# Cross-covariance attention: seventeen of the last eighteen stores issued from GpSimd's queue instead of SyncE's

## The chip, the cores and the metric

The kernel runs on one core of a Trainium2 chip. The metric is the device time of one execution in microseconds; the kernel before takes 128.43 us, the median of three runs. Engines are named as the profile names them: PE is TensorE, PEld its weight loads, DVE VectorE, ACT ScalarE, POOL GpSimd and SP SyncE. Sixteen DMA engines move data between HBM and the on-chip memory SBUF; any of several engines' queues can issue a transfer to them.

## The reference

Q, K and V have the shape (8, 12, 512, 64) in float32: 96 heads of 512 tokens by 64 features. Attention is between features, not tokens, so each head's attention matrix is 64x64.

```python
Q_norm = Q / (np.linalg.norm(Q, axis=-2, keepdims=True) + 1e-10)
K_norm = K / (np.linalg.norm(K, axis=-2, keepdims=True) + 1e-10)
attn = np.einsum('bhnd,bhne->bhde', Q_norm, K_norm)
attn = np.exp(attn - np.max(attn, axis=-1, keepdims=True))
attn = attn / (np.sum(attn, axis=-1, keepdims=True) + 1e-10)
return np.einsum('bhnd,bhde->bhne', V, attn).astype(np.float32)
```

Each of the three inputs and the output is 12.58 MB, so 50.3 MB cross between HBM and SBUF.

## The kernel before

The 96 heads are worked through in 24 units `u` of four heads, 12 pairs of units `s`, and 6 groups `w` of two pairs. For each pair, q and k are loaded in float32, cast to bfloat16 side by side (`cast_qk`, L213, DVE), and multiplied with themselves on PE (`grams`, L233), which gives the product of q and k together with their squared norms. From that come the norms (`squares`, `sums`, `powers`), the k side scaled by its norm (`scale_k`, L263, key `sc`, on POOL or DVE), a transposition (`logits`), the exponentials with the q side's norm as scale (`exps`, ACT) and the normalised attention in bfloat16 (`normalise`, L291).

V goes its own way: for each group it is loaded (`load_v`, key `lv`, L194 for a whole MB and L196 for the last one, which comes in two halves), cast to bfloat16 (`cast_v`, key `cv`, L170 on POOL and L168 on DVE), transposed on PE (`vtrans`, key `vt`, L302) and copied out of PSUM (`vcopy`, key `vc`). With both at hand, PE makes the output (`outs`, key `ou`, L319), four parts `x` for each pair; each part is copied to SBUF (`ocopy`, key `oc`, L166 on ACT, L168 on DVE) into the tile `so[s, i]`, of which a pair has two. There are 13 buffers for `so`. Each of the 24 tiles is 512 KB and is written to HBM by `store`, key `st`. I number the stores 2s + i, from 0 to 23. A store's rows in HBM are runs of 2 KB, two for each of 128 partitions.

Two stores have a form of their own. Number 19, (s, i) = (S - 3, 1), called `FEW`, is cut into four transfers (L204, L205) by partitions. Number 23, the last, is written in two halves with the keys `sh` and `st` (L457, L458), the first as soon as its first part is copied; its rows are then runs of 1 KB.

The order of all this isn't left to a scheduler: the class `Order` holds every piece of work with the engines it may run on, a planned cost, the pieces that it must come after (their ends) and behind (their beginnings), and a rank. `run` steps through a planned time, takes the piece that can begin first, or among those within 0.05 us the one of lowest rank, and gives each engine its program in that order. On the chip each engine then works in order, waiting at each instruction for what it needs. Transfers are pieces of the planned engine `DMA`, which means SP's queue: loads and stores stand there in one order, with up to 8 in flight (`QUEUE`). A store's rank is its place in the output plus `ST_LAG` (1.51), above the ranks of the loads, so that loads go first when both can.

The lines in question, L453 to L460: the stores, each behind the one before it. `S` is 12 and `W` 6; `BOTH` is 4, the pair from which DVE may help with the output copies.

Of the kernel before, what the change touches and what calls it, by code (L numbers as in the profile page):

```python
# [13 lines left out]
D = 64  # L14
# [88 lines left out]
def kernel(  # L103
# [7 lines left out]
    nc = tc.nc  # L111
# [3 lines left out]
    S = U // 2  # L115
    W = S // 2
# [3 lines left out]
    HELD, UNTIL = ("lk", 1, 1), ("cq", 0, 1)  # L120
    BOTH = S - 8
    FEW = (S - 3, 1)

# [9 lines left out]
    Of = out.rearrange("b h n d -> (b h n d)").rearrange(  # L135
        "(w r e i p x) -> w e i p r x", r=2, e=2, i=2, p=128, x=J * D)
# [25 lines left out]
    qk32, v32, vb, qkb, gram, scr, kq, n2, r8, kqs, rq, lg, ex, ab, vps, vt, po, so = ({} for _ in range(18))  # L162
# [26 lines left out]
    def load_v(w, r, c):  # L189
        if (w, r) not in v32:  # L190
            v32[w, r] = vp.tile([128, 2, T * D], F32, name="v32")
        o, i = v32[w, r], Vu[w, r].rearrange("p (c x) -> p c x", c=2)
        if c is None:
            nc.sync.dma_start(out=o.rearrange("p c x -> p (c x)"), in_=Vu[w, r])  # L194
        else:
            nc.sync.dma_start(out=o[:, c], in_=i[:, c])  # L196

    def store(s, i, k=None):
        rows = slice(None) if k is None else slice(k * (J // 2), (k + 1) * (J // 2))
        o = Of[s // 2, s % 2, i].rearrange("p r (j d) -> p r j d", d=D)  # L200
        if (s, i) == FEW:

            for a, b in ((0, 76), (76, 80), (80, 128)):
                nc.sync.dma_start(out=o[a:b, 0], in_=so[s, i][a:b, 0])  # L204
            nc.sync.dma_start(out=o[:, 1], in_=so[s, i][:, 1])  # L205
            return
        nc.sync.dma_start(out=o[:, :, rows], in_=so[s, i][:, :, rows])
# [151 lines left out]
    X = 1.29  # L359
    R = dict(cq=2.5, gr=2.471, sq=0.756, kq=1, rd=3.457, pw=3.5, sc=1, rq=1.9, lg=5, ex=1.1, nm=2.545, cv=1.165, vt=0.9, vc=1.1, ou=2, oc=0.9)  # L360
    BIAS = dict(sc=-0.6, kq=5, cv=1, vc=-0.3, oc=0.6)
    QK_PACE, V_FROM, V_PACE, ST_LAG = 0.631, 0.0377, 0.7486, 1.5133

    def v_at(v):
        return V_FROM + V_PACE * v / U

    def piece(key, engines, after, behind, rank, fn, *args):
        if key[0] in ("cv", "vc", "oc", "kq", "sc"):
            plan.add(key, engines, after, behind, rank, lambda eng: fn(eng, *args))
        else:  # L370
            plan.add(key, engines, after, behind, rank, lambda eng: fn(*args))

    def back(kind, i, n, *rest):
        return (kind, i - n, *rest) if i - n >= 0 else None
# [9 lines left out]
    for s in range(S):  # L384
        free = [back("cq", 2 * s + r, 2 * NB["qk"], x) for r in range(2) for x in range(2)]
        for r in parts(s):
            at = QK_PACE * (2 * s + (r or 0)) / U
# [4 lines left out]
    for u in range(U):  # L392
        s, r = divmod(u, 2)
# [17 lines left out]
    def turns(w):  # L411
        return [(q, f) for q in range(4) for f in ((0, 1) if w == W - 1 and q >= TAIL else (None,))]

    last, turned = None, None
    for w in range(W):
        both = 2 * w >= BOTH
        for r in range(2):
            halves = (0, 1) if (w, r) == (W - 1, 1) else (None,)
            n = 2 * w + r - NB["v"]
            for c in halves:  # L420
                free = [("cv", n // 2, n % 2, h) for h in range(2)] if n >= 0 else []
                piece(("lv", w, r, c), {"DMA": X if c is not None else 2 * X}, free, [last], v_at(4 * w + 2 * r + (c or 0)), load_v, w, r, c)
                last = ("lv", w, r, c)
            for c in range(2):
                free = [("vt", w - NB["vb"], *t) for t in turns(w - NB["vb"])] if w >= NB["vb"] else []
                piece(("cv", w, r, c), {"POOL": 1.15, "DVE": (0.72, BIAS["cv"])} if both else {"POOL": 1.15},
                      [("lv", w, r, c if len(halves) == 2 else None)] + free, [("cv", w, r, 0)] if c else [], R["cv"] + 0.01 * (4 * w + 2 * r + c), cast_v, w, r, c)
        for n, (q, f) in enumerate(turns(w)):
            if f is None:
                before = turns(w)[n - 1] if n else turns(w - 1)[-1] if w else None  # L430
                wait = [("vc", w if n else w - 1, *before)] if before else []
            else:
                wait = [("kq", S - 1)] + ([("vc", w, *turns(w)[n - 4])] if n >= 4 and turns(w)[n - 4][1] is not None else [])
            piece(("vt", w, q, f), {"PE": 0.6 if f is not None else 0.8}, [("cv", w, r, c) for r in range(2) for c in range(2)] + wait, [turned],
                  R["vt"] + 0.02 * w, vtrans, w, q, f)
            turned = ("vt", w, q, f)
            copies = {"ACT": 0.74 if f is not None else 1.31}
            if both:
                copies["DVE"] = (0.74 if f is not None else 1.42, BIAS["vc"])
            free = [("ou", 2 * (w - NB["vt"]) + e, x) for e in range(2) for x in range(4)] if w >= NB["vt"] else []  # L440
            piece(("vc", w, q, f), copies, [("vt", w, q, f)] + free, [("vc", w, *turns(w)[n - 1])] if n else [], R["vc"] + 0.02 * w, vcopy, w, q, f)
    for s in range(S):
        for x in range(4):
            i, k = divmod(x, 2)
            n = 4 * s + x - 2
            wait = [("oc", n // 4, n % 4)] if n >= 0 else []
            order = [("ou", s, x - 1) if x else back("ou", s, 1, 3)]
            piece(("ou", s, x), {"PE": 0.5}, [("vc", s // 2, *t) for t in turns(s // 2) if t[0] // 2 == k] + [("nm", s)] + wait, order, R["ou"] + 0.01 * s, outs, s, x)
            n = 2 * s + i - NB["so"]
            free = [("st", n // 2, n % 2)] if k == 0 and n >= 0 else []  # L450
            order = [("oc", s, x - 1) if x else back("oc", s, 1, 3)]
            piece(("oc", s, x), {"ACT": 0.6, "DVE": (0.68, BIAS["oc"])} if s >= BOTH else {"ACT": 0.6}, [("ou", s, x)] + free, order, R["oc"] + 0.01 * s, ocopy, s, x)
        for i in range(2):  # L453
            order = [("st", s, 0) if i else back("st", s, 1, 1)]
            if (s, i) == (S - 1, 1):

                piece(("sh", s, i), {"DMA": 0.67}, [("oc", s, 2)], order, v_at(2 * s + i) + ST_LAG, store, s, i, 0)  # L457
                piece(("st", s, i), {"DMA": 0.67}, [("oc", s, 3)], [("sh", s, i)], v_at(2 * s + i) + ST_LAG, store, s, i, 1)  # L458
            else:
                piece(("st", s, i), {"DMA": X}, [("oc", s, 2 * i), ("oc", s, 2 * i + 1)], order, v_at(2 * s + i) + ST_LAG, store, s, i)  # L460

    ahead = [loaded(x, 0, r) for r in range(2) for x in range(2)]
    held, passed = [], False
# [40 lines left out]
```

## Time and profile before

| | us |
|---|---|
| median of 3 runs (128.43, 128.66, 128.43) | 128.43 |
| the profiled execution | 128.57 |
| its span, first to last instruction | 126.8 |
| PE busy in the span | 79.6 (63%) |
| DVE busy | 91.5 (72%) |
| ACT busy | 72.6 (57%) |
| POOL busy | 36.3 (29%), 40 instructions |
| mean granted TensorE clock | 0.77 of full speed |
| moved by DMA over the span | 50.64 MB, mean 399 GB/s |

A busy share is an average over the whole span; no compute engine is above three quarters. The mean DMA rate has to be held against the rate in the middle of the span, where nothing starts or ends. Issuing a transfer isn't counted as busy time of the engine whose queue issues it, so SP has no busy time and POOL's 36.3 us are its casts and scalings. POOL issues no transfer in this kernel: SP issues all but two, which ACT issues at the start.

In views of single instructions, times are microseconds from the start of the span, and the name of an engine with a q behind it (SPq) is its queue: instructions that issue transfers, wait or synchronise. The views "DMA issues" give the time from the beginning of an issue to the last byte's receipt.

### The profile page before, as it was taken

What the parts mean: (1) busy time and instruction counts of PE and PEld (TensorE: products, weight loads), DVE (VectorE), ACT (ScalarE), POOL (GpSimd) and SP (SyncE); (2) the same over time, 40 slices, a digit from 0 to 9 for tenths busy, and PEclk for the clock granted to TensorE, in tenths of its full rate; (3) what the DMA queues carried; (4) which work ended last, traced back from release to release, by engine and by line L of the source; (5) the groups of instructions that cost most, each with busy time, mean ns of one, the idle gap of its engine ahead of it and who ended that gap; (6) DMA issues with size and microseconds to landing.
All of it is one profiled execution on the core that took longest, in us unless ns stands there. A gap on an engine that the chain in (4) does not pass through costs nothing.

```text
span 126.8 us, 4887 instructions
## 1 busy us (share of the span) xinstructions
PE 79.6 (63%) x2128; PEld 65.1 (51%) x2128; DVE 91.5 (72%) x141; ACT 72.6 (57%) x220; POOL 36.3 (29%) x40
## 2 busy tenths in 40 slices
PE   0064394895964779868574998696575898472000
PEld 0054372774843658656462886485464786361000
DVE  3254749939899399899896898999999799740000
ACT  4000441549688077786792788694748979974000
POOL 4005307300735903033065203223363270300000
PEclk9999655568599555899997569959999689755555
DMA  3999999999999999999999999999999999999993
GB/s 102 399 439 406 432 410 420 416 424 416 423 425 414 417 417 421 408 412 428 426 412 413 416 418 424 414 428 423 399 416 408 406 400 406 401 408 405 408 377 139
DMA packets 15629, 50.64 MB, mean 399 GB/s; under 512 B 1144, under 2 KB 1656, under 8 KB 14200
## 3 DMA queue, kind: packets, MB, share of 16 engines
q1 hardware_dynamic: 15320, 49.29, 96.5%
q10 hardware_dynamic: 288, 1.05, 2.1%
q8 instruction: 16, 0.26, 0.7%
q14 instruction: 5, 0.04, 0.1%
HBM read 37.75 MB, written 12.58 MB: 397 GB/s over the span
## 4 chain that ended last, share of the span: by engine, by line
DMA 36%; DVE 31%; PE 14%; ACT 5%; issue 4%; SPq 1%; DVEq 0%; ACTq 0%
DMA qk<-in_Q_dram 21%; DMA qk<-in_K_dram 15%; DVE qkb L213 11%; PE gram L233 8%; DVE scr L240 6%; DVE ab L291 4%; DVE vb L168 3%; PE po L319 3%; DVE vt L168 2%; DVE n L252 2%; PE vps L302 2%; ACT so L166 2%; ACT ex L282 1%; DVE so L168 1%; ACT kq L166 1%
## 5 line engine op out<-in xcount | busy, mean ns | idle before, releaser
L233 PE MATMUL gram<-qkb 32*128 32x128 bf16 (+1 forms) x1504 | 37.4, 263 | 19.7 <-DVE qkb L213 7.5
L233 PEld LDWEIGHTS <-qkb 32*128 32x128 bf16 (+1 forms) x1504 | 31.6, 118 | 24.2 <-DVE qkb L213 8.8
L213 DVE CAST qkb<-qk 128x1024 bf16<-128x1024 f32 x48 | 35.7, 766 | 8.8 <-DMA qk<-in_Q_dram 6.8
L170 POOL TENSOR_SCALAR vb<-v 128x1024 bf16<-128x1024 f32 x19 | 21.2, 1128 | 44.9 <-DMA v<-in_V_dram 35.0
L166 ACT COPY so<-po 128x512 f32<-128x512 f32 x45 | 24.8, 593 | 6.4 <-PE po L319 6.3
L166 ACT COPY vt<-vps 128x1024 bf16<-128x1024 bf16 (+1 forms) x18 | 17.8, 987 | 16.2 <-PE vps L302 16.2
L319 PE MATMUL po<-ab,vt 128*64 128x128 bf16 x384 | 21.2, 256 | 5.2 <-DVE ab L291 1.5
L302 PE MATMUL vps<-identb,vb 128*128 128x128 bf16 x192 | 18.0, 246 | 6.3 <-POOL vb L170 2.9
L263 POOL TENSOR_TENSOR kqs<-kq,r 64x512 f32<-64x512 f32 x12 | 13.8, 1147 | 26.9 <-ACT r L259 13.8
L240 DVE SCALAR_TENSOR_TENSOR scr<-gram,eye 64x512 f32<-64x512 f32 x24 | 16.5, 688 | 5.5 <-PE gram L233 5.2
L319 PEld LDWEIGHTS <-vt 128*64 128x64 bf16 x384 | 15.5, 130 | 9.6 <-issue 5.1
L302 PEld LDWEIGHTS <-vb 128*128 128x128 bf16 x192 | 13.4, 109 | 9.8 <-POOL vb L170 3.8
L282 ACT ACTIVATE ex<-lg,rq 128x64 f32<-128x64 f32 x48 | 14.5, 322 | 2.6 <-PE lg L276 2.3
L166 ACT COPY kq<-gram 64x512 f32<-64x512 f32 x12 | 7.0, 582 | 13.5 <-DVE scr L240 13.2
L291 DVE TENSOR_TENSOR ab<-ex,rinv 64x256 bf16<-64x256 f32 x24 | 13.8, 573 | 0.6
L282 ACT ACTIVATION_READ_ACCUMULATOR ex<-lg,rq 128x1 f32 x48 | 10.2, 213 | 0.0
L276 PE MATMUL lg<-eye,kqs 64*128 64x64 f32 x48 | 6.4, 259 | 4.2 <-POOL kqs L263 2.8
L252 DVE TENSOR_REDUCE n<-scr 128x8 f32<-128x512 f32 x12 | 8.1, 678 | 0.1
L168 DVE CAST vb<-v 128x1024 bf16<-128x1024 f32 x5 | 7.0, 1403 | 1.4 <-DMA v<-in_V_dram 1.3
L168 DVE COPY vt<-vps 128x1024 bf16<-128x1024 bf16 (+1 forms) x8 | 7.9, 1020 | 0.1
L276 PEld LDWEIGHTS lg<-eye,kqs 64*128 64x128 f32 x48 | 4.5, 156 | 6.0 <-POOL kqs L263 3.5
L288 DVE RECIPROCAL rinv<-esum 128x4 f32<-128x4 f32 x12 | 2.1, 172 | 2.7 <-ACT ex L282 2.5
(17 smaller groups left out, 15.9 us busy)
## 6 DMA issues: line engine op xcount, KB each, us to landing
v<-in_V_dram SPq DMA_DIRECT2D x11, 1024.0 KB, 17.0
out_dram<-so SPq DMA_DIRECT2D x22, 512.0 KB, 10.2
qk<-in_Q_dram SPq DMA_DIRECT2D x8, 1024.0 KB, 17.4
qk<-in_K_dram SPq DMA_DIRECT2D x8, 1024.0 KB, 17.4
qk<-in_Q_dram SPq DMA_DIRECT2D x8, 512.0 KB, 11.9
qk<-in_K_dram SPq DMA_DIRECT2D x6, 512.0 KB, 12.5
qk<-in_K_dram ACTq DMA_DIRECT2D x2, 512.0 KB, 7.4
v<-in_V_dram SPq DMA_DIRECT2D x2, 512.0 KB
```

What stands on the lines that cost most here:

```text
L166: nc.scalar.copy(o, i)
L168: nc.vector.tensor_copy(o, i)
L170: nc.gpsimd.tensor_scalar(out=o, in0=i, scalar1=1.0, scalar2=0.0, op0=ALU.mult, op1=ALU.add)
L213: nc.vector.tensor_copy(qkb[u][:, :, x * D:(x + 1) * D], qk32[s][:, x, r])
L233: nc.tensor.matmul(gram[s][:, h, r, 0], x, x, start=(t == 0), stop=(t == (T if u < WIDE else J) - 1))
L240: nc.vector.scalar_tensor_tensor(out=scr[s][half], in0=gram[s][half, :, :, 0, half].rearrange("p h r d -> p (h r) d"), scalar=1e-20, in1=e ...
L263: (nc.vector if eng == "DVE" else nc.gpsimd).tensor_tensor(out=kqs[s][HI], in0=kq[s][HI], in1=r8[s][HI, :, None].to_broadcast([D, 2 * HU, ...
L276: nc.tensor.transpose(l[:, h, :], kqs[s][HI, 2 * h:2 * h + 2].rearrange("p r d -> p (r d)"), eye2[HI])
L282: nc.scalar.activation(e[:, h, :], lg[s][:, h, :], AF.Exp, scale=rq[s][:, h:h + 1], accum_out=z[:, h:h + 1])
L291: nc.vector.tensor_tensor(out=a[half, :, half], in0=e[half], in1=ri[half, :, None].to_broadcast([D, HU, D]), op=ALU.mult,)
L302: nc.tensor.transpose(ps[:, c, n, :], vb[w][:, J * c + j].rearrange("p r d -> p (r d)"), identb)
L319: nc.tensor.matmul(po[s, x][e * D:(e + 1) * D, j].rearrange("p r d -> p (r d)"), v, ab[s][:, h, :])
```

## The change

The stores numbered 6 to 23, except 19, are issued from POOL's queue by a new function `soft`, whole, 23 included. Stores 0 to 5 and 19 stay on SP's queue with `store`. Each store is behind the one before it on the same queue. The first on POOL's queue, number 6, is behind the scaling of K of pair S - 3 = 9, and number 9 is also behind the last piece of the last cast of V, so that 6, 7 and 8 may stand ahead of that cast and the others may not. In the plan a store on POOL costs 0.75 us of POOL's time, with no flight time and no bound on how many are in flight. Everything else is as it was.

```diff
     FEW = (S - 3, 1)
+    SOFT = 6
...
+    def soft(s, i):
+
+        nc.gpsimd.dma_start(out=Of[s // 2, s % 2, i].rearrange("p r (j d) -> p r j d", d=D), in_=so[s, i])
...
+    stored = {"DMA": None, "POOL": ("sc", S - 3)}
     for s in range(S):
...
         for i in range(2):
-            order = [("st", s, 0) if i else back("st", s, 1, 1)]
-            if (s, i) == (S - 1, 1):
-
-                piece(("sh", s, i), {"DMA": 0.67}, [("oc", s, 2)], order, v_at(2 * s + i) + ST_LAG, store, s, i, 0)
-                piece(("st", s, i), {"DMA": 0.67}, [("oc", s, 3)], [("sh", s, i)], v_at(2 * s + i) + ST_LAG, store, s, i, 1)
+            done, eng = [("oc", s, 2 * i), ("oc", s, 2 * i + 1)], "POOL" if 2 * s + i >= SOFT and (s, i) != FEW else "DMA"
+            order, at = [stored[eng]], v_at(2 * s + i) + ST_LAG
+            if eng == "POOL":
+                if 2 * s + i == SOFT + 3:
+                    order.append(("cv", W - 1, 1, 1))
+                piece(("st", s, i), {"POOL": 0.75}, done, order, at, soft, s, i)
             else:
-                piece(("st", s, i), {"DMA": X}, [("oc", s, 2 * i), ("oc", s, 2 * i + 1)], order, v_at(2 * s + i) + ST_LAG, store, s, i)
+                piece(("st", s, i), {"DMA": X}, done, order, at, store, s, i)
+            stored[eng] = ("st", s, i)
```

## The prediction

> **What bounds the kernel now.** I read the DMA queues first.
>
> ```profile
> q1 hardware_dynamic: 15320, 49.29, 96.5%
> q8 instruction: 16, 0.26, 0.7%
> ```
>
> Each row is packets, MB and packet time as a share of 16 DMA engines over the 126.8 us span. One queue, SyncE's (SP's), fills the engines almost throughout. Then the rate by stretch (last columns: granted TensorE clock, DMA share, GB/s):
>
> ```profile
> 60.00:90.00 30.00, 22.60 (x602) 18.09 (x600) 26.99 (x40) 21.23 (x61) 8.81 (x8) 0.83 1.02 419
> ...
> 112.00:116.00 4.00, 2.57 (x38) 1.95 (x34) 0.30 (x1) 3.15 (x6) 0.00 (x0) 0.50 1.05 405
> 116.00:120.00 4.00, 0.00 (x0) 0.00 (x0) 0.00 (x0) 0.00 (x0) 0.00 (x0) 0.50 1.05 407
> ...
> 122.00:124.00 2.00, 0.00 (x0) 0.00 (x0) 0.00 (x0) 0.00 (x0) 0.00 (x0) 0.50 0.90 341
> 124.00:125.00 1.00, 0.00 (x0) 0.00 (x0) 0.00 (x0) 0.00 (x0) 0.00 (x0) 0.50 0.74 262
> 125.00:126.00 1.00, 0.00 (x0) 0.00 (x0) 0.00 (x0) 0.00 (x0) 0.00 (x0) 0.50 0.18 60
> ```
>
> 419 GB/s where loads dominate, 405 to 407 where only stores run, no computing after 116, and from 122 on the 16 engines run dry one after another: the first is done some 3 us before the last, at about 125.5. So the DMA engines that end last set the end, and computing has slack. Third, who issues what, near the change:
>
> ```profile
> 86.62 1.85 SPq L183 DMA_DIRECT2D qk<-in_K_dram  x1
> 89.11 3.12 SPq L196 DMA_DIRECT2D v<-in_V_dram  x2
> 92.99 17.06 SPq L207 DMA_DIRECT2D out_dram<-so  x14
> 110.83 2.75 SPq L204 DMA_DIRECT2D out_dram<-so  x3
> 114.53 0.37 SPq L205 DMA_DIRECT2D out_dram<-so  x1
> 115.86 4.78 SPq L207 DMA_DIRECT2D out_dram<-so  x5
> ```
>
> The columns are start, duration, line, operation, count. All loads are issued by 92.3; behind them stand 19 stores, numbers 5 to 23 (19 is the one in four pieces, 23 the one in halves). Last, GpSimd (POOL) and the last copies to `so`:
>
> ```profile
> 96.13 1.04 POOL L263 TENSOR_TENSOR kqs<-kq,r 64x512 f32<-64x512 f32 x1 [2.04 <-issue]
> 100.52 2.23 POOL L170 TENSOR_SCALAR vb<-v 128x1024 bf16<-128x1024 f32 x2 [3.35 <-DMA v<-in_V_dram]
> 102.83 1.09 POOL L263 TENSOR_TENSOR kqs<-kq,r 64x512 f32<-64x512 f32 x1
> 107.70 1.04 POOL L263 TENSOR_TENSOR kqs<-kq,r 64x512 f32<-64x512 f32 x1 [3.78 <-ACT r L259]
> ...
> 114.56 1.07 ACT L166 COPY so<-po 128x512 f32<-128x512 f32 x2 [0.24 <-PE po L319]
> ```
>
> POOL has one scaling of K at 96.13, the two last casts of V at 100.52, two more scalings, and is otherwise idle. The last output tile is complete at 115.63, 10 us before the data ends: that is the cover under everything below.
>
> **What the change removes.** SP loses 17 whole stores' issues, 5 and 19 staying (17 whole L207 issues, less store 5, is 16 removed, and the pair of halves of 23 as the 17th). SP's time costs nothing: it waits on its own queue, 10.2 us in all, for earlier stores to land. Stores 0 to 5 and all loads keep their order, and no moved store may begin ahead of the scaling at 96.13, so up to 96 us I expect no difference. Store 23 becomes one transfer. By the issue rows, a store issued at 118.43 landed 6.0 us later (124.4), the first half of 23, issued at 119.71, 5.4 us later (125.1): 0.7 us for a half against 1.3 for a whole, so 2 x 0.7 - 1.3 = -0.1 us. Bounds 0 and -0.1.
>
> **The transfer itself.** 524,288 B at 405 GB/s is 1.295 us a store, 17 make 22.0 us. No row shows a data transfer from POOL's queue. Bounds: at the rate of the stretch with loads (419) each is 0.043 us shorter, 17 x 0.043 = -0.7 us; at the poorest row of another queue, q8's (0.26 MB in 0.7% of 16 x 126.8 = 14.2 us of engine time, 18.5 GB/s each, 295 for sixteen), 8.91 MB take 30.2 us, +8.2. The nearest row is the same stores over SP's queue, so I take 0.
>
> **POOL's issue.** Call it e a store. SP's unblocked issue takes 0.37; its longest, with the queue full, 3.50. Nearest by engine is one pass of POOL over a tile, 1.04 to 1.13, and I take 1.05. Three issues from 97.2 (end of the scaling) end at 100.3, just ahead of the casts' 100.52: cost 0. At 0.37 also 0; at 3.50 they end at 107.7, and all of POOL moves by 7.2.
>
> During these issues VectorE is 2.71 us busy of the 3.30 between 97.20 and 100.50, 1.97 of it in the three casts of q and k. Here a rule speaks against the change: the Trainium skill, "SBUF — State Buffer", section "SBUF: two separate sides", says that a DMA issued from GpSimd has its descriptors written by GpSimd's cores, which VectorE's fp32 copies inside SBUF lock out of a shared port; it gives about 3.1 us for such a DMA beside one and 0.62 alone. If all three early stores met that, they would end at 97.2 + 9.3 = 106.5 by the page. No row here shows a software-issued DMA beside a cast; after 99.94 VectorE has no such cast left.
>
> **The casts of V.** The K load of 86.62 landed 12.5 us after its issue, at 99.1, and store 5, issued at 92.99, 9.9 after, at 102.9; so the second V half, ahead of that store, is in at about 101.6. The early stores now share the engines with it from about 98.2. If the queues take turns packet by packet, 4 KB of V against 2 KB of store, the 3.4 us left of V become up to 1.5 times that: +1.7, V at 103.3, the casts done at 103.3 + 1.1 = 104.4 instead of 102.75. TensorE's transposes of these V, the copies, the output matmuls and the last copy follow, 115.63 + 1.65 = 117.3. Behind the casts POOL's next scaling slips too, and a store ahead of the last scaling can add one e: 118.3. A last store issued then starts by 119.4 and takes 1.3; the engines hold work until 122 to 125.5. So 0, while the tail slips by less than about 4 us; beyond that each us is a us.
>
> **The gap.** While POOL casts, nobody issues stores. The engines that end last have in hand store 5 (102.9) and three early ones: 102.9 + 3 x 1.295 = 106.8, less some 0.3 for the receipt, 106.5. POOL: casts to 104.4, the scaling that already waits (1.09) to 105.5, store 9's issue to 106.55, first bytes perhaps 0.9 later (SP's first issue ended near 1.1 and the engines moved 12 GB/s between 1 and 2 us, 250 between 2 and 3): 107.45. Gap: about 0.9 us at worst order, 0 if the store goes ahead of the scaling or V is delayed less. The engines that end early have 3 us of slack for it. I take +0.5. From there POOL issues 14 stores and one scaling: 105.5 + 14 x 1.05 + 1.04 = 121.2, plus 0.9 and 1.3 is 123.4, inside the 125.5; one store per 1.05 us outruns 1.295.
>
> **The end.** From the last data (125.5) to the span's end stand 1.3 us of waits and clearing. POOL now has its own queue to close: 0 to +0.5 us (its longest drain here, 1.14, bounds it above); I take +0.1.
>
> **Sum.** -0.1 + 0 + 0 + 0.5 + 0.1 = +0.5 us on the profiled execution's own 128.57 (span 126.8 plus 1.8 around it): 129.07. The runs' median, 128.43, lies 0.14 below, so the forecast is **129.0**, range of its own 128.7 to 129.9.
>
> **Rivals.** *Faster (0.32):* packets from the new queue go at 419 GB/s, beside or without loads. For it: the engines sustain that with larger packets, and the new queue has its own descriptors; against: same engines, same 2 KB rows. It gives -0.7 - 0.1 with no gap on the slowest engines: 127.6. It decides from a store time of about 1.26 us on.
> The Trainium skill, "DMA: Bandwidth & Descriptors", section "Issuing engines are not separate DMA queues", denies it: all issuers share the same 16 engines and only issue time is saved; by that the term is 0.
>
> *POOL becomes the bound (0.13):* with e over 1.2 the last store starts too late: 105.5 + 14e + 1.04 + 0.9 + 1.3 passes 125.5 at e = 1.2. At 1.35 that is 14 x 0.15 = +2.1 on top of the 0.5: 131.0. For it: e is unseen, and POOL is in order, so a store that waits for its tile holds back a scaling. Against: POOL is idle 71% of the span and its plain passes take 1.05.
>
> *No difference (0.13):* no gap, the end as before: -0.1 + 0.1, 128.4. For it: bytes and engines are the same, and the bound is DMA.
>
> *Forecast (0.42).* So slower by over 0.2% has 0.42 + 0.13 = 0.55, faster 0.32, within 0.2% (0.26 us, about what a measurement of this kernel can tell from no change) 0.13. The range takes the faster case and POOL's up to e = 1.35: 127.5 to 131.0.
>
> **What would show it.** SP: no store between store 5 and store 19. The V halves landing after 101.6 and the casts after 100.52 show the sharing; the time between early landings of POOL's stores, 1.295 or not, decides the rate; the DMA share near 105 to 108 below 1.0 shows the gap; stretches with only stores should keep 405. I am wrong if stores run at 419 or clearly under 405, if e exceeds 1.2, or if the DMA share never dips and the end moves all the same.

## The result

The changed kernel takes 130.44 us (130.24 to 130.60, four runs), the kernel before in the same runs 128.55: a ratio of 1.0149, 95% interval 1.0136 to 1.0161, or 1.9 us slower. The forecast was 129.0, range 127.5 to 131.0: the direction is right and the range holds the time, but the +0.5 us should have been +1.9. The forecast's own range, 128.7 to 129.9, does not hold it.

First the DMA queues of the kernel after (packets, MB, share of 16 engines over its span of 128.8 us):

```profile
q1 hardware_dynamic: 10424, 40.37, 77.1%
q0 software_dynamic: 2448, 8.91, 17.5%
```

POOL's queue is the new row q0. Its 17 stores made 2,448 packets, 144 each, of which 16 are completions: so 128 packets of 4 KB for 512 KB, where SP's queue makes 256 of 2 KB. Unlike SP's, POOL's issues are counted as busy time: its page shows 57 instructions and 50.0 us, against 40 and 36.3 before. Then POOL's instructions (start, duration, line, operation, count):

```profile
95.93 1.04 POOL L268 TENSOR_TENSOR kqs<-kq,r 64x512 f32<-64x512 f32 x1 [2.12 <-issue]
96.92 2.35 POOL L201 DMA_DIRECT2D out_dram<-so  x3
100.43 1.03 POOL L171 TENSOR_SCALAR vb<-v 128x1024 bf16<-128x1024 f32 x1 [1.16 <-DMA v<-in_V_dram]
101.78 1.30 POOL L171 TENSOR_SCALAR vb<-v 128x1024 bf16<-128x1024 f32 x1 [0.32 <-ACT so L167]
103.02 0.77 POOL L201 DMA_DIRECT2D out_dram<-so  x1
103.86 1.03 POOL L268 TENSOR_TENSOR kqs<-kq,r 64x512 f32<-64x512 f32 x1
104.85 5.08 POOL L201 DMA_DIRECT2D out_dram<-so  x7
...
117.82 0.72 POOL L201 DMA_DIRECT2D out_dram<-so  x1 [0.59 <-ACT so L167]
```

An issue takes 0.72 us (the first 0.90), the three early ones end at 99.3, the last at 118.5; between 99.3 and 104.85 only one store is issued. The rate by stretch, the kernel after (last columns: granted clock, DMA share, GB/s):

```profile
100.00:102.00 2.00, 2.00 (x68) 1.58 (x55) 1.58 (x4) 1.90 (x8) 1.26 (x2) 1.00 1.02 408
102.00:104.00 2.00, 0.93 (x24) 0.77 (x22) 1.55 (x3) 0.78 (x4) 1.93 (x3) 1.00 0.93 373
104.00:106.00 2.00, 1.25 (x20) 0.91 (x14) 1.38 (x2) 1.11 (x2) 2.00 (x3) 0.91 0.86 345
106.00:108.00 2.00, 1.94 (x22) 1.74 (x21) 1.72 (x2) 1.95 (x11) 2.00 (x4) 0.50 0.95 377
116.00:118.00 2.00, 0.86 (x13) 0.43 (x8) 0.00 (x0) 1.38 (x3) 0.90 (x2) 0.50 1.01 342
122.00:124.00 2.00, 0.00 (x0) 0.00 (x0) 0.00 (x0) 0.00 (x0) 0.00 (x0) 0.50 1.03 419
124.00:125.00 1.00, 0.00 (x0) 0.00 (x0) 0.00 (x0) 0.00 (x0) 0.00 (x0) 0.50 0.78 320
125.00:126.00 1.00, 0.00 (x0) 0.00 (x0) 0.00 (x0) 0.00 (x0) 0.00 (x0) 0.50 0.38 156
126.00:127.00 1.00, 0.00 (x0) 0.00 (x0) 0.00 (x0) 0.00 (x0) 0.00 (x0) 0.50 0.15 61
```

Four things are to be seen against the kernel before, which ran at 396 to 409 GB/s from 100 to 122: a gap from 102 to 108; a dip at 116 to 118 with the engines busy all the same (share 1.01); 419 GB/s at 122 to 124, where all but 13 packets are those of POOL's stores; and a tail past 126 in which few engines still work. Last, the drains of SP's and POOL's queues at the end (count, shortest/median/longest ns, first and last start), the kernel before and then after:

```profile
L499 POOLq DRAIN  x3: 39/78/1144, 107.7 to 126.5; - x3
L499 SPq DRAIN  x3: 7/7/7, 126.0 to 126.3; - x3
```

```profile
L507 SPq DRAIN  x3: 7/7/7, 127.5 to 128.3; - x3
L507 POOLq DRAIN  x3: 40/102/10254, 117.8 to 128.6; - x3
```

After, POOL's first drain starts at 117.8 and takes 10.25 us, to 128.05, 0.55 after SP is ready. From the last completion record of a transfer to the span's end it is 126.78 - 125.83 = 0.95 us before and 128.83 - 127.30 = 1.53 after. So of 2.05 us of span, 1.47 lie before the last landing and 0.58 behind it.

### The profile page after: what moved, and what is told of

It reads as the page before. It is cut to its first block, busy times and chain, and to the rows that moved or that the text cites. A ratio compares the mean times of both kernels' runs of the same rounds, so it can differ in the third digit from the quotient of the medians.

```text
span 128.8 us, 4877 instructions
## 1 busy us (share of the span) xinstructions
PE 77.1 (60%) x2128; PEld 62.5 (48%) x2128; DVE 93.4 (72%) x141; ACT 72.8 (57%) x220; POOL 50.0 (39%) x57
## 3 DMA queue, kind: packets, MB, share of 16 engines
q0 software_dynamic: 2448, 8.91, 17.5%
q10 hardware_dynamic: 288, 1.05, 2.1%
## 4 chain that ended last, share of the span: by engine, by line
DVE 29%; DMA 20%; PE 15%; POOL 9%; issue 9%; ACT 8%; POOLq 1%; SPq 0%; DVEq 0%; ACTq 0%
DMA qk<-in_Q_dram 20%; DVE qkb L218 14%; PE gram L238 10%; POOL out_dram L201 6%; DVE scr L245 6%; DVE ab L296 5%; ACT vt L167 3%; PE vps L307 2%; ACT ex L287 2%; POOL kqs L268 2%; PE po L324 2%; DVE n L257 1%; PE lg L281 1%; ACT so L167 1%; DVE vb L169 1%
## 5 line engine op out<-in xcount | busy, mean ns | idle before, releaser
L238 PE MATMUL gram<-qkb 32*128 32x128 bf16 (+1 forms) x1504 | 35.4, 255 | 25.7 <-DVE qkb L218 9.4
L238 PEld LDWEIGHTS <-qkb 32*128 32x128 bf16 (+1 forms) x1504 | 29.8, 114 | 30.3 <-DVE qkb L218 12.5
L218 DVE CAST qkb<-qk 128x1024 bf16<-128x1024 f32 x48 | 37.5, 807 | 7.4 <-DMA qk<-in_Q_dram 5.9
L171 POOL TENSOR_SCALAR vb<-v 128x1024 bf16<-128x1024 f32 x19 | 22.4, 1187 | 37.1 <-DMA v<-in_V_dram 36.7
L324 PE MATMUL po<-ab,vt 128*64 128x128 bf16 x384 | 20.7, 247 | 5.3 <-issue 2.4
L324 PEld LDWEIGHTS <-vt 128*64 128x64 bf16 x384 | 14.6, 124 | 10.0 <-issue 5.8
L296 DVE TENSOR_TENSOR ab<-ex,rinv 64x256 bf16<-64x256 f32 x24 | 15.5, 645 | 0.6
L201 POOL DMA_DIRECT2D out_dram<-so x17 | 12.6, 741 | 3.0 <-ACT so L167 3.0
L169 DVE CAST vb<-v 128x1024 bf16<-128x1024 f32 x5 | 5.1, 1023 | 0.1
```

The lines of the kernel that those rows point to most:

```text
L169: nc.vector.tensor_copy(o, i)
L171: nc.gpsimd.tensor_scalar(out=o, in0=i, scalar1=1.0, scalar2=0.0, op0=ALU.mult, op1=ALU.add)
L201: nc.gpsimd.dma_start(out=Of[s // 2, s % 2, i].rearrange("p r (j d) -> p r j d", d=D), in_=so[s, i])
L218: nc.vector.tensor_copy(qkb[u][:, :, x * D:(x + 1) * D], qk32[s][:, x, r])
L238: nc.tensor.matmul(gram[s][:, h, r, 0], x, x, start=(t == 0), stop=(t == (T if u < WIDE else J) - 1))
L296: nc.vector.tensor_tensor(out=a[half, :, half], in0=e[half], in1=ri[half, :, None].to_broadcast([D, HU, D]), op=ALU.mult,)
```

## Experiments

The orders of PE, DVE and ACT are the same in all of these kernels and in both of the case; only POOL's and SP's queues differ. The ratio is to the kernel before in the same runs.

**Store 19 whole, on POOL's queue.**

```diff
-            done, eng = [("oc", s, 2 * i), ("oc", s, 2 * i + 1)], "POOL" if 2 * s + i >= SOFT and (s, i) != FEW else "DMA"
+            done, eng = [("oc", s, 2 * i), ("oc", s, 2 * i + 1)], "POOL" if 2 * s + i >= SOFT else "DMA"
```

> The kernel after, with store 19 whole and on POOL's queue like the others (18 of the last 18). Theory A (the gap at 103 to 106 us takes from the engines their different leads, and then store 19's four pieces put some 1.6 us of extra rows on four engines that no longer lead, which therefore end last): the four engines lose that, the others gain 0.4, the last landing moves from 127.3 to about 126.5, time 129.6 against the 130.44 of the kernel after. Rival B (the uneven store does nothing; what is lost is lost by slower packets while POOL makes descriptors): 130.4 within 0.15.

129.58 us, ratio 1.0087 (1.0074 to 1.0100): 0.86 us less than after, as theory A had it. The four pieces are the first rows of 76, 4 and 48 partitions and then the second rows of all 128. The trace has a completion record from each of the 16 DMA engines for a whole store, but for the pieces of 76 and of 4 partitions only four late ones each. If each piece is split evenly over its engines, four engines carry 19 + 1 + 3 + 8 = 31 rows and the others 11, where a whole store gives each 16; at 84 ns a row that is an estimated 1.3 us more for the four and 0.4 us less for the others. The records, sorted, in us:

```
store 18 (before):       116.55 116.65 116.94 117.09 117.30 117.74 118.13 118.26 119.26 119.34 119.50 119.53 119.55 119.57 119.64 119.65
last store (before):     122.66 122.78 123.21 124.27 124.66 125.01 125.36 125.44 125.46 125.59 125.63 125.66 125.67 125.74 125.75 125.83
store 16 (after):        115.61 115.67 116.19 116.28 116.53 116.55 116.56 116.58 116.60 116.61 116.64 116.68 116.76 116.81 117.22 117.31
last store (after):      124.56 124.94 124.95 125.00 125.00 125.02 125.04 125.61 125.84 125.96 126.04 126.08 126.75 126.82 127.21 127.30
last store (few_whole):  124.56 124.63 125.37 125.45 125.51 125.53 125.54 125.55 125.73 125.77 125.85 125.91 125.92 126.09 126.12 126.20
```

Store 18 is the last ahead of the pieces in the kernel before, store 16 in the kernel after. Before, the engines are 3.1 us apart there; after, only 1.7, and behind the pieces four stand apart at the end, 0.7 to 1.2 us behind the twelfth. With the store whole they don't.

**More or fewer stores ahead of the casts.** For six, stores 9 to 11 are put in front of the first of the two casts in the finished order:

```diff
-    for (emit, eng), (_, _, key, _) in zip(plan.run(), plan.order):
+    steps = list(zip(plan.run(), plan.order))
+    early = [t for t in steps if t[1][2] in [("st", n // 2, n % 2) for n in range(SOFT + 3, SOFT + 6)]]
+    steps = [t for t in steps if t not in early]
+    at = [t[1][2] for t in steps].index(("cv", W - 1, 1, 0))
+    steps[at:at] = early
+    for (emit, eng), (_, _, key, _) in steps:
```

For none:

```diff
-                if 2 * s + i == SOFT + 3:
+                if 2 * s + i == SOFT:
```

> The kernel after, with six of POOL's stores ahead of the last casts of V instead of three; all other engines' orders are as in the kernel after. Theory A: the gap in the DMA share at 103 to 106 us closes, the engines keep their leads, store 19's uneven pieces fill them again: about 129.7 although the casts begin 0.9 us later. Rival B (the gap falls only on engines that have slack): 130.4 within 0.15. Rival C (the later casts push the last tiles out): above 130.6.

> The kernel after, with none of POOL's stores ahead of the last casts of V (store 6 comes after them). Theory A: the gap grows by what three stores bridged, DMA stands still on nearly all engines from about 102.6 to 104, and the end moves by 1 to 2 us: 131.4 to 132.4. Rival B (gaps fall on slack): 130.4 within 0.3.

Six ahead: 129.19 us, ratio 1.0050 (1.0028 to 1.0072). None ahead: 134.22, ratio 1.0460 (1.0436 to 1.0484), twice what theory A allowed. With none ahead, DMA nearly stops:

```profile
100.00:102.00 2.00, 2.00 (x85) 1.74 (x73) 1.04 (x3) 1.95 (x9) 1.25 (x2) 1.00 0.49 189
102.00:104.00 2.00, 1.40 (x28) 0.93 (x24) 1.95 (x3) 1.27 (x6) 1.93 (x3) 1.00 0.09 36
```

The fewer stores ahead, the later the end; that the gap would fall on slack is refuted. But the twelve runs with six ahead spread from 128.39 to 130.09, those of no other kernel over more than 1.02 us; in its profiled run POOL's first store was issued at 98.01, not 96.92, and the share was still 0.99 to 1.00 at 104 to 108, so the gap was not quite closed there. Nor were the leads quite kept: at store 16 the engines were 2.0 us apart, against 3.1 where store 19 is whole as well.

**Both edits, and store 19 whole on SP's queue.** To six ahead, the edit of the first experiment; or this, so that 19 stays on SP's queue in one piece:

```diff
-        if (s, i) == FEW:
+        if FEW is None:
```

> Six of POOL's stores ahead of the last casts of V and store 19 whole on POOL's queue: both edits of the two kernels before in one. Theory A (store 19's four pieces harm only where the gap has taken the leads of the four engines): with the leads kept, the pieces help, so leaving them out costs, and this is 0.3 us or more slower than the 129.19 with six ahead alone: 129.5 to 130. Rival B (the pieces harm beside POOL's queue whatever the leads): the two gains of 0.9 and 1.25 us add up, about 128.4.

> Six of POOL's stores ahead of the casts, and store 19 whole on SP's queue (with six ahead alone it stands there in four pieces). If the dip at 116 to 118 us and its cost come from the uneven pieces beside POOL's queue, the dip goes and the time is that of store 19 whole on POOL's queue, 128.9 to 129.0. If two queues at work together are the cause, the dip stays and the time is that of six ahead, 129.2 or more.

128.94 us (1.0031, 1.0019 to 1.0043) and 128.89 (1.0029, 1.0017 to 1.0040). Neither theory of the first had it: the pieces neither help nor cost a full 0.9 here; leaving them out gains 0.25, within the spread of six ahead. The second settles the dip: with store 19 whole there is none, on either queue. The same three stretches, 102 to 108, 108 to 114 and 114 to 119, first for the kernel before:

```profile
102.00:108.00 6.00, 5.12 (x93) 4.12 (x88) 5.89 (x8) 5.04 (x19) 2.14 (x3) 0.95 1.05 403
108.00:114.00 6.00, 3.83 (x56) 3.21 (x58) 3.44 (x9) 5.07 (x18) 0.74 (x1) 0.62 1.05 404
114.00:119.00 5.00, 1.01 (x16) 0.73 (x15) 0.00 (x0) 1.39 (x3) 0.00 (x0) 0.50 1.05 407
```

then for store 19 whole but the gap open:

```profile
102.00:108.00 6.00, 3.98 (x50) 3.24 (x51) 4.27 (x7) 3.61 (x13) 5.93 (x8) 0.73 0.90 357
108.00:114.00 6.00, 4.39 (x57) 3.57 (x55) 4.72 (x10) 4.61 (x19) 5.46 (x7) 0.50 1.02 404
114.00:119.00 5.00, 3.04 (x42) 2.25 (x39) 0.55 (x2) 3.46 (x6) 2.91 (x4) 0.50 1.02 395
```

then six ahead, with the pieces:

```profile
102.00:108.00 6.00, 5.09 (x92) 4.09 (x93) 3.87 (x7) 3.85 (x9) 5.83 (x8) 0.86 1.01 404
108.00:114.00 6.00, 3.56 (x68) 2.79 (x67) 5.33 (x11) 5.91 (x27) 4.51 (x6) 0.99 1.02 401
114.00:119.00 5.00, 2.77 (x39) 1.86 (x34) 0.33 (x1) 3.23 (x6) 2.91 (x4) 0.50 1.02 380
```

and six ahead with store 19 whole on SP's queue:

```profile
102.00:108.00 6.00, 4.67 (x49) 3.65 (x50) 3.37 (x5) 3.58 (x13) 5.92 (x8) 0.58 1.03 414
108.00:114.00 6.00, 4.58 (x77) 3.57 (x76) 4.76 (x11) 5.74 (x22) 3.47 (x5) 0.85 1.03 414
114.00:119.00 5.00, 1.18 (x24) 0.73 (x23) 0.00 (x0) 2.06 (x4) 2.18 (x3) 0.77 1.03 415
```

The gap takes the first stretch, the pieces beside POOL's queue the last, and where neither is, the stores run at 414 GB/s, above the 403 to 407 of the kernel before. The kernel after has 365, 400 and 365 in them.

**The pieces in the kernel before.** Store 19 is whole on SP's queue:

```diff
-    FEW = (S - 3, 1)
+    FEW = None
```

> The kernel before with store 19 whole on SP's queue. If the four pieces serve to fill four engines that lead by 1.2 us and more by then, leaving them out costs: the last engines get 0.4 us more, 128.9 against 128.46. If they serve nothing: 128.4.

128.87 us, ratio 1.0028 (1.0018 to 1.0039): as expected, the pieces are worth 0.36 us there. So the right base for the queue change alone is 128.87, and six ahead with store 19 whole, 128.94, is the same kernel but for POOL's queue and the whole last store.

**The pieces elsewhere.** To six ahead: store 5, the last on SP's queue ahead of POOL's, is cut up, and 19 is whole on POOL's.

```diff
-    FEW = (S - 3, 1)
+    FEW = (2, 1)
```

> Six of POOL's stores ahead of the casts; the store in four pieces is number 5, the last on SP's queue, instead of 19, which is whole on POOL's. With the pieces out of the time in which POOL's queue works, the dip to 343 GB/s at 116 to 118 us should go. If the dip costs time, 128.7 or less; if it falls on engines with slack, 129.2 as with six ahead.

128.59 us, ratio 1.0008 (0.9998 to 1.0017): the dip is gone and it is as fast as the kernel before, with runs from 128.38 to 129.14, of which the profiled one is the slowest. That is 0.35 us less than with store 19 whole and no pieces, as much as the pieces are worth in the kernel before.

**The end.** To the kernel after: stores 22 and 23 on SP's queue, or only the last store on POOL's.

```diff
-            done, eng = [("oc", s, 2 * i), ("oc", s, 2 * i + 1)], "POOL" if 2 * s + i >= SOFT and (s, i) != FEW else "DMA"
+            done, eng = [("oc", s, 2 * i), ("oc", s, 2 * i + 1)], "POOL" if 2 * s + i >= SOFT and (s, i) != FEW and s < S - 1 else "DMA"
```

```diff
-    SOFT = 6
+    SOFT = 23
```

> The kernel after, with stores 22 and 23 on SP's queue, whole. Theory A: the 0.5 us between SP's last wait and POOL's drain at the end (127.5 to 128.1) is POOL's drain waiting for its own last store; with SP's stores last the drain is done before, so the time between the last landing and the end falls from 1.5 to 1.0 us: 129.9. Rival B (closing POOL's queue costs that whenever it was used): 130.4.

> The kernel after with only store 23 on POOL's queue, whole; stores 6 to 22 stand on SP's queue as before. Theory A: POOL's drain at the end waits for its own last store and ends 0.5 us after SP's, so the time from the last landing to the end grows from 0.95 to 1.5 us: 128.9 to 129.0 against 128.46. Rival B (the end costs nothing where POOL issued only one): 128.4.

130.45 us (1.0154, 1.0138 to 1.0171) and 128.57 (1.0001, 0.9993 to 1.0010). By the times, rival B in the first and no cost in the second. The traces say why. With only the last store on POOL's queue, that store was issued at 115.77, before SP, whose queue was full, had issued 20 to 22 (116.11 to 118.67), and landed by 122.88, ahead of them:

```profile
L507 POOLq DRAIN  x3: 40/93/7230, 115.7 to 126.6; - x3
L507 SPq DRAIN  x3: 7/7/7, 126.0 to 126.3; - x3
```

A drain of 7.23 us from 115.7 ends at 123.0, 3 us before SP needs it, and the end keeps its 0.95 us. With the last two on SP's, POOL's drain ended at 126.03, before the last landing (127.04), but SP then went through eight more waits of 0.06 us in its fixed list of semaphores: 1.33 us to the end. So theory A's mechanism holds, but moving a store gains only what SP's list leaves.

The drain ends some time after the last landing of POOL's own stores, and over all the traces that time follows the number of stores that POOL issued: 0.09 us for 1, 0.55 for 12, 0.67 for 15, 0.71 for 16, 0.75 for 17 and 0.79 for 18, so about 0.04 us a store. By that, one store alone would cost little even as the last to land; no run tests it.

**The last store whole, alone**, in the kernel before:

```diff
-            if (s, i) == (S - 1, 1):
-
-                piece(("sh", s, i), {"DMA": 0.67}, [("oc", s, 2)], order, v_at(2 * s + i) + ST_LAG, store, s, i, 0)
-                piece(("st", s, i), {"DMA": 0.67}, [("oc", s, 3)], [("sh", s, i)], v_at(2 * s + i) + ST_LAG, store, s, i, 1)
-            else:
-                piece(("st", s, i), {"DMA": X}, [("oc", s, 2 * i), ("oc", s, 2 * i + 1)], order, v_at(2 * s + i) + ST_LAG, store, s, i)
+            piece(("st", s, i), {"DMA": X}, [("oc", s, 2 * i), ("oc", s, 2 * i + 1)], order, v_at(2 * s + i) + ST_LAG, store, s, i)
```

> The kernel before with store 23 whole instead of in two halves. The prediction's term: -0.1 us, 128.4 against 128.5. Rival: the first half's early issue is worth something, 128.6 or more.

128.41 us against 128.54, ratio 0.9990 (0.9981 to 0.9998): -0.13 us, as priced. In the traces, though, only 0.05 us of it lies ahead of the last landing; the time behind that falls from 0.95 to 0.85 us, since the last store's wait now stands last in SP's list.

**All of it together.** Six ahead, the pieces in store 5, store 19 on POOL's queue, and stores 22 and 23, or 18 to 23, on SP's. To the kernel with the pieces in store 5, for the first (with `S - 3` for the second):

```diff
-            done, eng = [("oc", s, 2 * i), ("oc", s, 2 * i + 1)], "POOL" if 2 * s + i >= SOFT and (s, i) != FEW else "DMA"
+            done, eng = [("oc", s, 2 * i), ("oc", s, 2 * i + 1)], "POOL" if 2 * s + i >= SOFT and s < S - 1 else "DMA"
```

> Six ahead, the pieces in store 5, store 19 whole on POOL's queue (128.59 so far), and stores 22 and 23 whole on SP's queue. If 0.6 us of the end are POOL's drain waiting for its own last store, the time from the last landing to the end falls from 1.55 to 1.0 us: 128.0 to 128.2, faster than the kernel before. If SP's slower packets and its list of waits give it back: 128.5.

> As six5_two_sp, with stores 18 to 23 on SP's queue and 6 to 17 on POOL's. The end as short, but four stores more at 405 instead of 419 GB/s (+0.2 us): 128.2 to 128.4. If two queues at work together lose rate, 128.6 or more.

128.01 us, ratio 0.9962 (0.9948 to 0.9977), and 128.25, ratio 0.9976 (0.9966 to 0.9985). The first is faster than both kernels of the case. The second lies in its expected range for another reason than the expected one: its last landing comes only 0.08 us later (125.31), but four waits of SP's list still follow it, and the time behind it is 1.14 us, not 0.94. In the first, SP is through its list 0.09 us after the last landing (125.23), so the end is short:

```profile
L512 POOLq DRAIN  x3: 40/102/11434, 114.0 to 125.9; - x3
L512 SPq DRAIN  x3: 7/7/7, 125.3 to 125.7; - x3
```

POOL's drain, 11.43 us from 113.96, ends at 125.4, less than 0.1 after SP is ready, and the span 0.94 after the last landing.

## Why the prediction was right, and where its size went

The times add up. Kernel before with store 19 whole, 128.87; POOL's queue without gap or pieces, 128.94 (+0.07); the gap, 129.58 (+0.64); the pieces behind the gap, 130.44 (+0.86). Less the 0.36 that the pieces give the kernel before (128.51 in that run), that is +1.9. These are differences between runs in which the kernel before took 128.46 to 128.55, so each is good to about 0.1 us.

That the stated range holds 130.44 is luck. Its top, 131.0, was put there for POOL as the bound, with 1.35 us for an issue, and that didn't happen; the forecast's own range ended at 129.9.

- **SP's issues at 0, no difference up to 96 us, the whole store at -0.1:** right in size; the scaling that releases POOL's stores starts at 95.93 against 96.13, the whole store alone measured -0.13. But the prediction looked for that in the transfer, and most of it lies in SP's waits.
- **The transfer at 0:** mis-sized. The last stores land 1.25 us apart, not 1.29. With neither gap nor pieces the last landing is at 125.63, against 126.25 in the kernel before with store 19 whole: 0.6 us earlier, near the lower bound of -0.7 and by the faster rival's mechanism, a higher rate. The gain is paid back at the end (1.57 us behind the last landing against 0.97), which the rival left out; hence the +0.07. That all issuers share 16 engines (the Trainium skill, "DMA: Bandwidth & Descriptors", section "Issuing engines are not separate DMA queues") agrees with the trace, in which no stretch of stores passes 426 GB/s; that only issue time is saved does not, since a store took 0.04 us less. It goes with the size of the packets: one of 4 KB took 159 ns (the median, on SP's own loads as well), two of 2 KB 168.
- **POOL's issue at 1.05:** 0.72, so under the 1.2 from which POOL would become the bound; that rival is out.
- **The lock of the port** (the Trainium skill, "SBUF — State Buffer", section "SBUF: two separate sides"): the page's 3.1 us are for a DMA issued from GpSimd beside such a copy of VectorE's. No issue here came near that; the longest beside a cast took 1.16. But in most of these traces one of the two takes longer where they meet; that the port is the reason is not shown. In the kernel after, the early issues took 0.90, 0.73 and 0.72 us, no longer than with DVE idle (0.90 for the first of the queue, where only the last store is on it), and DVE's casts took longer; first before, then after:

```profile
97.45 1.29 DVE L213 CAST qkb<-qk 128x1024 bf16<-128x1024 f32 x2
97.37 1.69 DVE L218 CAST qkb<-qk 128x1024 bf16<-128x1024 f32 x2
```

With six ahead it can be the other way round. Where store 19 is whole on POOL's queue, the six early issues took 4.52 us and the casts beside them 0.82 to 0.95 us each; in the profiled run of six ahead alone the casts took 0.68 to 0.72 and the issues 5.16, two of them 1.16 and 1.09:

```profile
97.03 4.52 POOL L201 DMA_DIRECT2D out_dram<-so  x6
98.01 5.16 POOL L201 DMA_DIRECT2D out_dram<-so  x6
```

- **V later by 1.7:** wrong. The last half of V landed at 101.71 (101.6 before) and the casts ended at 103.08, not 104.4. What the early stores held up was SP's store 5, whose last engine ended at 105.50 instead of 102.94.
- **The gap at +0.5:** that there is a gap was right, what it costs was not, and this is the step that failed: "The engines that end early have 3 us of slack for it." I priced the gap only for the engines that end last, and on those there was none: the last record of store 8 is at 106.61 and that of store 9 at 107.84, a store's usual time later. Store 9 went ahead of the scaling and V was hardly delayed, the case that the prediction itself priced at 0. The engines that were ahead stood still and lost their leads, and that was not free. First, store 19 puts extra rows on four engines that the kernel counts on being ahead: 0.86 us, of which 0.25 stood with six ahead as well, where the leads were not quite kept; how much of it is lost leads and how much the pieces beside POOL's queue isn't separated. Second, there are 0.64 us with store 19 whole. Up to store 16 the last record is where it is without a gap (116.83 against 116.84), but the last store lands at 126.20 against 125.63, and packets of 4 KB that started between 116.8 and 122 took 165 ns on average, against 161. Together that is 1.5 us in place of 0.5, by a way that the prediction didn't have, so the right sign of its 0.5 is luck. I described store 19 in the kernel and never asked what its four pieces were for.
- **The end at +0.1:** mis-sized, +0.58, beyond its bounds of 0 to 0.5. I looked at the length of a drain and not at when it can end: POOL's waits for its own last store, that store is the last of all to land, and the drain then takes about 0.04 us for each of the 17 stores.

Two points stay open. Between 108 and 119 the share is above 1 while the rate is 404 and 395 with the gap and 411 and 410 without, store 19 whole in both: packets of 4 KB take longer after a gap (166 ns on average in this time, against 162). In the trace eight engines then complete a store within 0.2 us of one another (109.14 to 109.31 in the kernel after), where without a gap they are strung out; that engines in step get into one another's way is my reading, not shown. And why the pieces slow the engines only beside POOL's queue stays open too: at 116 to 118 in the kernel after, packets of 4 KB took 180 ns on average and those of 2 KB 129; with six ahead and store 19 whole on SP's queue 160 and 84.

## What to carry to other kernels

Sixteen DMA engines behind one queue are sixteen machines with their own backlogs: here a gap in which the slowest lost nothing still took the others' leads, and a transfer shaped to use those leads then landed on engines without one. Before moving stores, ask of every odd-shaped transfer what imbalance it was cut for, and whether that survives. If a second queue is worth having, feed it far enough ahead of the first in-order work that blocks it, and let the other queue issue the last stores.

## What the runs showed of the hardware

- The same 512 KB store makes 256 packets of 2 KB on SP's queue and 128 of 4 KB on POOL's; a store every 1.25 us on POOL's (419 GB/s) against 1.29 (405 to 407). A packet of 4 KB took 159 ns, one of 2 KB 84.
- A store's issue took 0.72 us of POOL, the first of the queue 0.90. Beside DVE's casts of q and k, in most of the traces either the issue grew (to 1.16 and 1.09) or the cast did (from 0.69 to between 0.82 and 0.97).
- POOL's drain at the end waited for the last landing of its own stores and took about 0.04 us more for each store that POOL had issued: 0.09 us for one, 0.75 for 17 (127.30 to 128.05). In the kernel after, the time behind the last landing was 0.58 us longer than before.
